# Expert weights in pages of 2 MB, each partition's 16 KB in one piece, gate and up side by side

## The chip, the cores and the metric

The kernel runs on one core of a Trainium2 chip. A core has TensorE (PE, matrix products), VectorE (DVE), ScalarE (ACT), GpSimd (POOL) and SyncE (SP, which here issues all transfers), an SBUF of 128 partitions, and 16 DMA engines that carry weights from HBM into it. The metric is the device time of one execution in microseconds (us).

## The reference

A block of attention (two kinds side by side) with a mixture of experts, and a second block of a state-space layer, a recurrent layer and two convolutional feed-forward layers; 256 tokens of 1024 features, all in fp32. The change concerns the experts of the first block:

```
N_EXPERTS = 16
EC_CAPACITY_FACTOR = 2
D_FF_EXPERT = 2 * D_MODEL

def expert_choice_ffn(h, w_router, w_gate, w_up, w_down):
    B, S, D = h.shape
    cap = EC_CAPACITY_FACTOR * S // N_EXPERTS
    aff = jax.nn.softmax((h @ w_router).astype(jnp.float32), axis=-1)
    gate, idx = lax.top_k(jnp.swapaxes(aff, 1, 2), cap)
    bidx = jnp.arange(B)[:, None, None]
    xe = h[bidx, idx]
    hid = (jax.nn.silu(jnp.einsum('becd,edf->becf', xe, w_gate))
           * jnp.einsum('becd,edf->becf', xe, w_up))
    ye = jnp.einsum('becf,efd->becd', hid, w_down) * gate[..., None].astype(h.dtype)
    return jnp.zeros_like(h).at[bidx, idx].add(ye)
```

Each of 16 experts takes 32 tokens. Its three weights, gate and up of 1024 x 2048 and down of 2048 x 1024, are 8 MB each in fp32, so the experts read 384 MB (a MB is 2^20 bytes here), each number once.

## The kernel before

The program is recorded through tile pools: a pool hands out buffers ("tiles") by tag, and a tile that takes the place of an older one makes its first writer wait until the older one's readers are done. A scheduler then orders each engine's instructions. Eight completion semaphores (DMAHW0 to DMAHW7 in the listings) are used in turn for transfers, so that a transfer waits until the eighth before it has landed.

**Pages.** Expert weights are loaded as pages of 1 MB, 8 KB for each of 128 partitions, by `load_epage` (L828 to L835). A page of gate or up is 128 rows of 2048 numbers, so that each partition gets its 8 KB as one piece. A page of down is 256 rows of 1024 numbers, two rows for each partition, two pieces of 4 KB. An expert has 24 pages: eight of gate, eight of up, eight of down.

**The ring.** The pages go into a ring of 21 places, in the order in which the room of the first block comes free: 2 in the pool `swap` (room that also holds the first half of the attention scores, `half`), 9 in `pages3`, the 5 of the pool `pages` through which the kernel loads its other weights, 4 in `pages2`, 1 in `pages4`. `pages2` to `pages4` lie where the first block kept its split weights and attention data. Page 21 goes where page 0 was, once the products with page 0 are done.

**The products of an expert** (L1065 to L1106). `xeT` holds the features of the expert's tokens along partitions. For each of the eight pages of gate, four products of 32 tokens by 512 columns go into four row groups of one accumulator, `gu0`; fp32 products run as two passes, so the profile counts eight. The same for up into `gu1`. ScalarE applies SiLU to `gu0` (L1079), VectorE multiplies by `gu1` (L1080), four transposes turn the result (`hidt`, L1083), ScalarE copies it (`hidT`, L1085), and the eight pages of down follow (`dn`, L1096). VectorE takes the result out of the accumulator with the gains (`ye`, L1099), and four products with a selection matrix add it, gated, to the tokens (`ca`, L1102). Ahead of the first expert the router picks tokens and `gather` fills `xeT` for two experts; for the other 14 it does so beside the second expert's products.

```
    ring = [(swap, "swap", 2)] * 2 + [(pages3, "page3", NP3)] * NP3 + [(pages, "page", NPAGE)] * NPAGE + \
        [(pages2, "page2", 4)] * 4 + [(pages4, "page4", 1)]
```

Of the kernel before, what the change touches and what calls it, by code (L numbers as in the profile page):

```python
# [9 lines left out]
F32 = mybir.dt.float32  # L10
# [9 lines left out]
S = 256  # L20
# [4 lines left out]
# ---------------------------------------------------------------- host layout  # L25
# [10 lines left out]
for _n, _k in COLS:  # L36
# [5 lines left out]
    # of the first block only  # L42
    ("thr", 1), ("mask0", 192), ("mask1", 192), ("invf", 1), ("sgn", 1), ("sel4", 4), ("maskp1", 128), ("maskp2", 128),
    # of all of it
# [9 lines left out]
# relative-position buckets in the order of rising key-minus-query distance, and  # L54
# the distance from which each holds
# [35 lines left out]
def column(a):  # L91
    """[..., n] vectors as columns of 128: [128, rows * n / 128]"""
    a = np.asarray(a)
    return a.reshape(-1, 128).T
# [5 lines left out]
def layout(inp):  # L100
    """the arrays of setup_inputs() as the program takes them"""
    o = {}
    cols = []
    for name, n in COLS:
        a = np.asarray(inp["b_ada" if name == "b_ada0" else name])
        if name == "b_ada0":
            # first 2048 numbers as [p, chunk, group], feature = group * 512 + chunk * 128 + p
            a = a[:, :2048].reshape(4, 4, 128).transpose(1, 0, 2)
# [42 lines left out]
    o["b_ada"] = np.asarray(inp["b_ada"]).reshape(3, 2048)  # L151
    o["a_log"] = np.asarray(inp["ssd_a_log_2"]).reshape(-1)
    skip = {"w_router", "b_ada", "w_uq", "w_ukv", "rel_bias", "positions"} | {n for n, _ in COLS}
# [7 lines left out]
def tile_model(ctx, tc, A, out):  # L161
# [28 lines left out]
    # ---------------------------------------------------------------- helpers  # L190
# [11 lines left out]
    def wpage(w, c0, n, k0=0, k=8):  # L202
        """columns c0..c0+n of rows 128*k0..128*(k0+k) of a weight"""
        return page([128, k, n], w[k0 * 128:(k0 + k) * 128, c0:c0 + n].rearrange("(k p) n -> p k n", p=128))

    def split(v, pl=None, tag="w", bufs=None, lo=None, parts=1):
        """v = hi + lo exactly, each of 12 significant bits"""
# [16 lines left out]
    def three(ps, a, b, first, last):  # L224
        """ps += a^T b for split a and b (lists over the contraction of (hi, lo) pairs)"""
# [11 lines left out]
    def inv_rms(pl, v, n, extra=None):  # L237
        """1 / sqrt(v / n + EPS) for v [128, m], the sums of n squares (m > 1: extra is None)"""
# [21 lines left out]
    def sumsq(eng, a, scratch, v):  # L260
        """v = the sums of squares over the free axis of a"""
# [7 lines left out]
    def inv_root(pl, v, n, extra=None, bias=None):  # L269
        """1 / sqrt((v + extra) / n + EPS) for v [128, 1]; bias [128, 1] takes the place of extra / n + EPS"""  # L270
# [8 lines left out]
    def root_table(pl, v):  # L279
        """the square root's table ahead of its use, from the time at which v is there"""  # L280
# [8 lines left out]
    # x1 / residual, expert inputs and rows live through several phases  # L289
    epsc = const.tile([128, 1], F32, name="epsc")  # L290
    dve.memset(epsc, EPS)
    s2c = const.tile([128, 16], F32, name="s2c")     # 1+sc2 (times gain), sh2 as columns

    # ================================================================= block 1
# [4 lines left out]
    # in the order in which their places come free  # L299
    PW = [192, 128, 128]  # L300
    # scores of the dilated heads: the first half of the heads where the first pages of the experts go
    P = [[], [], []]
    half = [swap.tile([128, 2048], F32, name="half", tag="swap", bufs=2) for _ in range(2)]
# [27 lines left out]
    W_Q0 = 704                                      # first column of the dilated heads  # L331
# [19 lines left out]
    # conditioning: one row of 6 * D numbers, four groups of columns side by side  # L351
# [4 lines left out]
    modc = act_p.tile([128, 4, 4], F32, name="modc")        # [p, chunk, group]  # L356
# [17 lines left out]
    # the rest of it, needed much later: products on the vector engine, sums over partitions at the end  # L374
# [8 lines left out]
    def mods_cols(c0, name):  # L383
        """8 * 128 of the sums as columns"""
# [6 lines left out]
    def mods_end2():  # L391
        dve.scalar_tensor_tensor(s2c[:, 0:8], mods_cols(0, "sc2"), 1.0, C("g_norm_ffn", 0, 8), ALU.add, ALU.mult)
        gt2.append(rows2.tile([128, 512], F32, name="gt2"))     # first half of the features over the second
# [11 lines left out]
    def mod_cols(j0):  # L405
        """[128, 2, 4] view of the columns of one D-vector: feature = (j - j0) * 512 + c * 128 + p"""
        return modc[:, :, j0:j0 + 2].rearrange("p c j -> p j c")
# [9 lines left out]
    # x over its norm  # L417
# [6 lines left out]
    # positions and relative-position bias, bias and band mask together  # L424
# [15 lines left out]
    def rel_bias(g, t, b):  # L440
        """bias and mask of 16 keys in each quarter of the keys of a query tile"""
# [21 lines left out]
    def tick(n=1):  # L463
        """a piece of the work that only has to be done sometime before it is needed"""
# [6 lines left out]
    # rotation angles, features along partitions (two heads of 64)  # L471
    def angles():
# [5 lines left out]
        # turns, as a multiple of 4096 and a rest  # L478
# [23 lines left out]
    def to_T(src, scol, bcol, hi, lo, pl, tpf, full=None):  # L502
        """columns of src (natural, 2 token tiles) to [features, tokens], scaled per feature, split"""
# [25 lines left out]
    # x over its norm, features along partitions  # L529
# [46 lines left out]
    # ------------------------------------------------------------ projections  # L576
    pace = [0, 1]

    def proj_T(pg, ps_of):
        """pg [128, 8, n]: for each 128 columns, [columns, tokens]"""  # L580
# [8 lines left out]
    def proj_N(pg, ps_of, tok):  # L589
        """pg [128, 8, n], or its split: [tokens, n] for the two tiles of tokens"""  # L590
# [42 lines left out]
    # gates, first half  # L633
# [18 lines left out]
    def softmax_rows(ps_view, p, den):  # L652
        """p = exp(MSC * (s - max)) for [128, 2, n] scores; den their sums"""
# [75 lines left out]
    # ------------------------------------------------------ dilated attention  # L729
# [47 lines left out]
    # weights of the three groups, in the natural order of tokens with heads along partitions  # L777
# [41 lines left out]
    # the pages of the experts, one after the other, in a ring of places  # L819
# [794 lines left out]
```

## Time and profile before

| | |
|---|---|
| median of 3 runs | 2344.3 us (2344.11 to 2346.31) |
| span of the profiled execution | 2346.6 us |
| PE busy | 2015.6 us, 86% |
| DVE, ACT, POOL busy | 937.9, 760.3, 277.5 us |
| DMA | 645.36 MB in 249,592 packets, mean 275 GB/s |
| expert pages | 3 x 128 transfers of 1024 KB, median 20 us from issue to landing |

The span runs from the first to the last instruction of one profiled execution; the page gives no other time for that execution. The experts take from about 483 us (first product) to 1408 us (last product). In the page's forms, "a<-b,c" means that an instruction writes tile a and reads b and c, and in the lists of products "x8" counts instructions that stand together. The share of the DMA is the busy time of the 16 DMA engines over the stretch; since records of neighbouring packets overlap a little, it can exceed 1. A product's busy time is partly modelled.

### The profile page before, as it was taken

What the parts mean: (1) busy time and instruction counts of PE and PEld (TensorE: products, weight loads), DVE (VectorE), ACT (ScalarE), POOL (GpSimd) and SP (SyncE); (2) the same over time, 40 slices, a digit from 0 to 9 for tenths busy, and PEclk for the clock granted to TensorE, in tenths of its full rate; (3) what the DMA queues carried; (4) which work ended last, traced back from release to release, by engine and by line L of the source; (5) the groups of instructions that cost most, each with busy time, mean ns of one, the idle gap of its engine ahead of it and who ended that gap; (6) DMA issues with size and microseconds to landing.
All of it is one profiled execution on the core that took longest, in us unless ns stands there. A gap on an engine that the chain in (4) does not pass through costs nothing. (4 is left out here: it accounts for less than half of the span.)

```text
span 2346.6 us, 32322 instructions
## 1 busy us (share of the span) xinstructions
PE 2015.6 (86%) x13779; PEld 1398.2 (60%) x13779; DVE 937.9 (40%) x1353; ACT 760.3 (32%) x1070; POOL 277.5 (12%) x209
## 2 busy tenths in 40 slices
PE   7999999998766776667676669999999999899998
PEld 5989999842111111111111119887899998799998
DVE  7866664321000000000000007665556566765565
ACT  2445453310000000000000006564555457654544
POOL 0100032000000000000000003112322222222222
PEclk9999999999676667766766779999999999999999
DMA  8358765799999999999999997333466546455652
GB/s 315 109 185 264 229 221 188 287 370 417 417 417 417 417 417 417 417 417 417 417 417 417 417 402 235 97 113 122 162 190 188 181 143 202 144 180 182 193 182 82
DMA packets 249592, 645.36 MB, mean 275 GB/s; under 512 B 10596, under 2 KB 164580, under 8 KB 213606
## 3 DMA queue, kind: packets, MB, share of 16 engines
q1 hardware_dynamic: 249448, 643.29, 73.7%
q8 instruction: 108, 1.77, 0.3%
q14 instruction: 36, 0.29, 0.0%
HBM read 641.94 MB, written 1.05 MB: 274 GB/s over the span
## 5 line engine op out<-in xcount | busy, mean ns | idle before, releaser
L219 DVE TENSOR_TENSOR wl<-page,wh 128x2048 fp32r<-128x2048 f32 (+2 forms) x191 | 431.9, 2266 | 307.6 <-ACT wh L218 307.4
L1075 PE MATMUL gu<-epage,xeT 128*32 128x512 f32 x2048 | 355.6, 785 | 149.5 <-DMA epage<-in_w_up 91.4
L218 ACT CAST wh<-page 128x2048 fp32r<-128x2048 f32 (+2 forms) x191 | 356.6, 1873 | 340.1 <-PE up L231 147.7
L1075 PEld LDWEIGHTS gu<-epage,xeT 128*32 128x32 f32 x2048 | 52.1, 121 | 429.2 <-DMA epage<-in_w_up 225.0
L230 PE MATMUL up<-hh,wh 128*128 128x256 f32 x960 | 271.7, 283 | 0.0
L232 PE MATMUL up<-hh,wl 128*128 128x256 f32 x960 | 271.7, 283 | 0.0
L231 PE MATMUL up<-hl,wh 128*128 128x256 f32 x960 | 271.7, 283 | 0.0
L1096 PE MATMUL dn<-epage,hidT 128*32 128x512 f32 x1024 | 186.3, 837 | 94.3 <-DMA epage<-in_w_down 82.7
L1080 DVE TENSOR_TENSOR hid<-hid,gu 128x512 f32<-128x512 f32 x16 | 11.0, 688 | 479.4 <-PE gu L1075 479.4
L231 PEld LDWEIGHTS up<-hl,wh 128*128 128x128 f32 x960 | 184.2, 192 | 1.0
L230 PEld LDWEIGHTS up<-hh,wh 128*128 128x128 f32 x960 | 184.2, 192 | 1.0
L232 PEld LDWEIGHTS up<-hh,wl 128*128 128x128 f32 x960 | 184.2, 192 | 0.0
L1079 ACT ACTIVATE hid<-gu 128x512 f32<-128x512 f32 x16 | 9.6, 597 | 528.4 <-PE gu L1075 528.4
L1096 PEld LDWEIGHTS dn<-epage,hidT 128*32 128x32 f32 x1024 | 27.3, 128 | 233.6 <-DMA epage<-in_w_down 201.2
L274 POOL TENSOR_SCALAR iq<-ssq 128x1 f32<-128x1 f32 x16 | 8.0, 500 | 1013.3 <-ACT x L263 975.3
L1099 DVE TENSOR_TENSOR ye<-dn,gt 128x512 f32<-128x512 f32 x16 | 11.1, 692 | 289.2 <-PE dn L1096 289.2
L1085 ACT COPY hidT<-hidt 128x512 f32<-128x512 f32 x16 | 9.4, 586 | 312.0 <-PE hidt L1083 312.0
L230 PE MATMUL qk<-hh,wh 128*128 128x256 f32 x384 | 109.9, 286 | 0.0
L231 PE MATMUL qk<-hl,wh 128*128 128x256 f32 x384 | 109.0, 284 | 0.0
L232 PE MATMUL qk<-hh,wl 128*128 128x256 f32 x384 | 108.7, 283 | 0.0
L1243 DVE SCALAR_TENSOR_TENSOR cv<-up,cols,cv 128x255 f32<-128x255 f32 x240 | 98.7, 474 | 12.5 <-ACT cv L1238 12.5
L232 PE MATMUL ca<-wh,hdl 128*128 128x512 f32 x256 | 100.1, 391 | 0.4 <-POOL hdl L219 0.4
(506 smaller groups left out, 3956.2 us busy)
## 6 DMA issues: line engine op xcount, KB each, us to landing
epage<-in_w_gate SPq DMA_DIRECT2D x128, 1024.0 KB, 20.0
epage<-in_w_up SPq DMA_DIRECT2D x128, 1024.0 KB, 19.8
epage<-in_w_down SPq DMA_DIRECT2D x128, 1024.0 KB, 19.9
page<-in_ffn_w_up SPq DMA_DIRECT2D x64, 1024.0 KB, 5.7
page<-in_w_in SPq DMA_DIRECT2D x46, 1024.0 KB, 5.4
page<-in_ffn_w_down SPq DMA_DIRECT2D x32, 1024.0 KB, 4.9
page<-in_w_ada SPq DMA_DIRECT2D x24, 1024.0 KB, 8.8
page<-in_ssd_w_in SPq DMA_DIRECT2D x20, 1024.0 KB, 5.4
```

The costliest lines, as they stand in the source:

```text
L218: act.copy(hi[p_], v[p_])
L219: (lo or dve).tensor_tensor(lw[p_], v[p_], hi[p_], ALU.subtract)
L230: pe.matmul(ps, lhsT=ah, rhs=bh, start=first and k == 0, stop=False)
L231: pe.matmul(ps, lhsT=ah, rhs=bl, start=False, stop=False)
L232: last_mm[0] = pe.matmul(ps, lhsT=al, rhs=bh, start=False, stop=last and k == n - 1)
L1075: pe.matmul(ps[32 * j:32 * j + 32, :], lhsT=xeT[:, k, 32 * e:32 * e + 32], rhs=pg[:, 0, 512 * j:512 * j + 512], start=(k == 0), stop=(k == 7))
L1079: act.activation(out=hid, in_=gu[0], func=AF.Silu)
L1080: dve.tensor_tensor(hid, hid, gu[1], ALU.mult)
L1085: act.copy(hT, pt.rearrange("p (c j s) -> p c j s", c=4, j=4))
L1096: pe.matmul(pd[32 * q:32 * q + 32, :], lhsT=hT[:, 2 * c2 + cp, j, :], rhs=pg[:, cp, 512 * n:512 * n + 512], start=(b == 0), stop=(b == 7))
L1099: dve.tensor_tensor(ye, pd, gt2, ALU.mult)
L1243: dve.scalar_tensor_tensor(y[:, c, o:], ps[:, 256 * c:256 * c + S - o], wcol(c, j), y[:, c, o:], ALU.mult, ALU.add)
```

## The change

The weights are laid out anew before the launch: `w_gu` holds, for each expert and each 128 rows, gate's 2048 and up's 2048 numbers of a row side by side, 16 KB; `w_dn` holds, for each expert and each 512 rows of down, the four rows of a partition side by side, 16 KB. A page is now 2 MB, 12 to an expert: eight of gate and up together, four of down. The ring has 10 places of 2 MB: 1 in `swap`, 4 in `pages3`, 2 that are each two of the five 1 MB tiles of the pool `pages`, 2 in `pages2`, 1 in `pages4`. A page is loaded in one transfer, but in two halves of 1 MB (8 KB of each partition) where its place is a pair of `pages` tiles, and for the last page of all. Gate's and up's products with a page follow each other, into both accumulators. `half`, the two tiles of attention scores in `swap`, become two halves of one tile. (Comments were taken out as well, which moves line numbers.)

```diff
+    gu = np.stack([np.asarray(inp[n])[0].reshape(16, 8, 128, 2048) for n in ("w_gate", "w_up")], axis=3)
+    o["w_gu"] = gu.reshape(16, 8, 128, 4096)
+    o["w_dn"] = np.asarray(inp["w_down"])[0].reshape(16, 4, 4, 128, 1024).transpose(0, 1, 3, 2, 4).reshape(16, 4, 128, 4096)
...
-    half = [swap.tile([128, 2048], F32, name="half", tag="swap", bufs=2) for _ in range(2)]
+    half = swap.tile([128, 4096], F32, name="half", tag="swap", bufs=1)
+    half = [half[:, 0:2048], half[:, 2048:4096]]
...
-    ring = [(swap, "swap", 2)] * 2
+    ring = [(swap, "swap", 1)]
     expert_pages = []
     for e in range(NE):
-        for w in (A["w_gate"], A["w_up"]):
-            expert_pages += [(w[0, e, 128 * k:128 * k + 128, :], 1) for k in range(8)]
-        expert_pages += [(A["w_down"][0, e, 256 * b:256 * b + 256, :], 2) for b in range(8)]
+        expert_pages += [A["w_gu"][e, k] for k in range(8)] + [A["w_dn"][e, b] for b in range(4)]
...
         pl, tag, nb = ring[cnt[0] % len(ring)]
-        src, a = expert_pages[cnt[0]]
+        src = expert_pages[cnt[0]]
         cnt[0] += 1
-        t = pl.tile([128, 2048], F32, name="epage", tag=tag, bufs=nb)
-        v = t.rearrange("p (a n) -> p a n", a=a)
-        last_dma[0] = sync.dma_start(out=v, in_=src.rearrange("(a p) n -> p a n", p=128))
+        if pl is pages:
+            v = [pl.tile([128, 2048], F32, name="epage", tag=tag, bufs=nb) for _ in range(2)]
+        else:
+            t = pl.tile([128, 4096], F32, name="epage", tag=tag, bufs=nb)
+            v = [t[:, :2048], t[:, 2048:]]
+        if pl is pages or cnt[0] == len(expert_pages):
+            for i in range(2):
+                last_dma[0] = sync.dma_start(out=v[i], in_=src[:, 2048 * i:2048 * i + 2048])
+        else:
+            last_dma[0] = sync.dma_start(out=t, in_=src)
         return v
...
-    pages2 = w2.enter_context(tc.tile_pool(name="pages2", bufs=4, reuse_waits="tile"))
-    pages3 = w2.enter_context(tc.tile_pool(name="pages3", bufs=NP3, reuse_waits="tile"))
+    pages2 = w2.enter_context(tc.tile_pool(name="pages2", bufs=2, reuse_waits="tile"))
+    pages3 = w2.enter_context(tc.tile_pool(name="pages3", bufs=4, reuse_waits="tile"))
     pages4 = w2.enter_context(tc.tile_pool(name="pages4", bufs=1, reuse_waits="tile"))
-    ring = [(swap, "swap", 2)] * 2 + [(pages3, "page3", NP3)] * NP3 + [(pages, "page", NPAGE)] * NPAGE + \
-        [(pages2, "page2", 4)] * 4 + [(pages4, "page4", 1)]
+    ring = [(swap, "swap", 1)] + [(pages3, "page3", 4)] * 4 + [(pages, "page", NPAGE)] * 2 + \
+        [(pages2, "page2", 2)] * 2 + [(pages4, "page4", 1)]
...
-        gu = []
-        for i, w in enumerate((A["w_gate"], A["w_up"])):
-            ps = cm(f"gu{i}")
-            for k in range(8):
-                pg = epage()
+        gu = [cm(f"gu{i}") for i in range(2)]
+        for k in range(8):
+            pg = epage()
+            for i in range(2):
                 for j in range(4):
-                    pe.matmul(ps[32 * j:32 * j + 32, :], lhsT=xeT[:, k, 32 * e:32 * e + 32],
-                              rhs=pg[:, 0, 512 * j:512 * j + 512], start=(k == 0), stop=(k == 7))
-            gu.append(ps)
+                    pe.matmul(gu[i][32 * j:32 * j + 32, :], lhsT=xeT[:, k, 32 * e:32 * e + 32],
+                              rhs=pg[i][:, 512 * j:512 * j + 512], start=(k == 0), stop=(k == 7))
...
-        for b in range(8):
+        for j in range(4):
             pg = epage()
-            j, c2 = divmod(b, 2)
-            for cp in range(2):
-                for n in range(2):
-                    q = 2 * n + cp
-                    pe.matmul(pd[32 * q:32 * q + 32, :], lhsT=hT[:, 2 * c2 + cp, j, :],
-                              rhs=pg[:, cp, 512 * n:512 * n + 512], start=(b == 0), stop=(b == 7))
+            for c2 in range(2):
+                for cp in range(2):
+                    for n in range(2):
+                        q = 2 * n + cp
+                        o = 1024 * cp + 512 * n
+                        pe.matmul(pd[32 * q:32 * q + 32, :], lhsT=hT[:, 2 * c2 + cp, j, :], rhs=pg[c2][:, o:o + 512],
+                                  start=(j == 0 and c2 == 0), stop=(j == 3 and c2 == 1))
```

SyncE's list where the ring fills for the first time, before: the last places of `page3` and `pages`, then the five of `pages2` and `pages4`, then the first page that waits for products of an expert.

```order
L834 DMA epage<-in_w_up 128x2048 [waits DMAHW0_49]
L834 DMA epage<-in_w_up 128x2048 [waits DMAHW1_49,DVE_49]
L834 DMA epage<-in_w_up 128x2048 [waits DMAHW2_49,DVE_49]
L834 DMA epage<-in_w_down 128x2x1024 [waits DMAHW3_49,PE_49]
L834 DMA epage<-in_w_down 128x2x1024 [waits DMAHW4_49]
L834 DMA epage<-in_w_down 128x2x1024 [waits DMAHW5_49]
L834 DMA epage<-in_w_down 128x2x1024 [waits DMAHW6_49]
L834 DMA epage<-in_w_down 128x2x1024 [waits DMAHW7_49,DVE_49]
L834 DMA epage<-in_w_down 128x2x1024 [waits DMAHW0_49,PE_49]
```

The same place of SyncE's list after the change, where `in_w_gu` is gate and up and `in_w_dn` is down:

```order
L845 DMA epage<-in_w_gu 128x4096 [waits DMAHW2_49]
L843 DMA epage<-in_w_gu 128x2048 [waits DVE_49]
L845 DMA epage<-in_w_gu 128x4096 [waits DMAHW4_49,DVE_49,PE_49]
L845 DMA epage<-in_w_dn 128x4096 [waits DMAHW5_49]
L845 DMA epage<-in_w_dn 128x4096 [waits DMAHW6_49,DVE_49]
L845 DMA epage<-in_w_dn 128x4096 [waits DMAHW7_49,PE_49]
```

Three transfers of 2 MB instead of five of 1 MB fill `pages2` and `pages4`, and one tile of `pages` is filled ahead of them where two were; the next row waits for the products with page 0 in both.

TensorE's list around the end of an expert's gate and up, before: the last two pages of up (one accumulator, `gu_6110`), the transposes, the first page of down.

```order
L1075 MATMUL gu_6110<-epage,xeT 32x512 [waits DMAHW1_49]
L1075 MATMUL gu_6110<-epage,xeT 32x512 x3
L1075 MATMUL gu_6110<-epage,xeT 32x512 [waits DMAHW2_49]
L1075 MATMUL gu_6110<-epage,xeT 32x512 x3
L1083 MATMUL hidt<-kc,hid 128x128 [waits DVE_49]
L1083 MATMUL hidt<-kc,hid 128x128 x3
L1096 MATMUL dn<-epage,hidT 32x512 [waits DMAHW3_49,Activation_49]
L1096 MATMUL dn<-epage,hidT 32x512 x3
```

The same place after the change, with gate's accumulator `gu_5854` and up's `gu_5855`:

```order
L1084 MATMUL gu_5854<-epage,xeT 32x512 [waits DMAHW7_49]
L1084 MATMUL gu_5854<-epage,xeT 32x512 x3
L1084 MATMUL gu_5855<-epage,xeT 32x512 x4
L1084 MATMUL gu_5854<-epage,xeT 32x512 [waits DMAHW0_49]
L1084 MATMUL gu_5854<-epage,xeT 32x512 x3
L1084 MATMUL gu_5855<-epage,xeT 32x512 x4
L1091 MATMUL hidt<-kc,hid 128x128 [waits DVE_49]
L1091 MATMUL hidt<-kc,hid 128x128 x3
L1105 MATMUL dn<-epage,hidT 32x512 [waits DMAHW1_49,Activation_49]
L1105 MATMUL dn<-epage,hidT 32x512 x7
```

One wait for a landed page now stands ahead of eight products instead of four, and gate's sum is complete only with the last page, four products ahead of up's.

SyncE's list at the end of the experts, before: the last pages, three small loads, and the first weights of the second block.

```order
L834 DMA epage<-in_w_down 128x2x1024 [waits DMAHW1_49,PE_49]
L834 DMA epage<-in_w_down 128x2x1024 [waits DMAHW2_49,PE_49]
L1124 DMA cols_8231<-in_cols 128x766 [waits DMAHW3_49,PE_49]
L1114 DMA row<-in_g_final 128x1024 [waits DMAHW4_49]
L1114 DMA rowa<-in_norm_mix_pre 128x1024 [waits DMAHW5_49]
L199 DMA page<-in_ssd_w_dt 128x8x128 [waits DMAHW6_49,PE_49]
L199 DMA page<-in_ssd_w_in 128x8x256 [waits DMAHW7_49,PE_49]
```

The same place after the change:

```order
L845 DMA epage<-in_w_dn 128x4096 [waits DMAHW7_49,PE_49]
L843 DMA epage<-in_w_dn 128x2048 [waits DMAHW0_49,PE_49]
L843 DMA epage<-in_w_dn 128x2048 [waits DMAHW1_49]
L1133 DMA cols_7923<-in_cols 128x766 [waits DMAHW2_49,PE_49]
L1123 DMA row<-in_g_final 128x1024 [waits DMAHW3_49]
L1123 DMA rowa<-in_norm_mix_pre 128x1024 [waits DMAHW4_49]
L203 DMA page<-in_ssd_w_dt 128x8x128 [waits DMAHW5_49]
L203 DMA page<-in_ssd_w_in 128x8x256 [waits DMAHW6_49,PE_49]
```

The order is the same; the last page is in two transfers, and the first weights of the second block no longer wait for TensorE.

## Rows read from the trace of the kernel before

**Rows 1.** The page: GB/s moved by DMA in 40 slices of 58.7 us

```profile
GB/s 315 109 185 264 229 221 188 287 370 417 417 417 417 417 417 417 417 417 417 417 417 417 417 402 235 97 113 122 162 190 188 181 143 202 144 180 182 193 182 82
```

**Rows 2.** The DMA queue's own waits: total us, times, longest us

```profile
SPq L834 <- DMA epage<-in_w_gate: 255.3, 121, 3.4
SPq L834 <- DMA epage<-in_w_down: 135.5, 80, 3.4
SPq L834 <- DMA epage<-in_w_up: 133.6, 75, 2.5
SPq L834 <- PE gu L1075: 79.4, 66, 16.7
```

**Rows 3.** Groups of instructions, 547 to 1404 us: busy us, mean ns, idle before

```profile
L1075 PE MATMUL gu<-epage,xeT 128*32 128x512 f32 x1824 | 323.4, 808 | 149.5 <-DMA epage<-in_w_up 91.4 <-DMA epage<-in_w_gate 57.8
L1096 PE MATMUL dn<-epage,hidT 128*32 128x512 f32 x956 | 178.2, 853 | 93.7 <-DMA epage<-in_w_down 82.7 <-ACT hidT L1085 11.0
L1102 PE MATMUL ca<-ye,sel 128*128 128x512 f32 x112 | 75.3, 833 | 11.4 <-DVE ye L1099 11.4
```

**Rows 4.** Timeline within one expert: start us, us, instruction, idle before and releaser

```profile
820.43 0.60 ACT L1079 ACTIVATE hid<-gu 128x512 f32<-128x512 f32 x1 [37.72 <-PE gu L1075]
...
823.40 1.94 PE L1075 MATMUL gu<-epage,xeT 128*32 128x512 f32 x8 [0.46 <-DMA epage<-in_w_up]
...
838.31 1.93 PE L1075 MATMUL gu<-epage,xeT 128*32 128x512 f32 x8 [0.55 <-DMA epage<-in_w_up]
...
840.38 0.69 DVE L1080 TENSOR_TENSOR hid<-hid,gu 128x512 f32<-128x512 f32 x1 [32.88 <-PE gu L1075]
...
842.98 4.13 PE L1096 MATMUL dn<-epage,hidT 128*32 128x512 f32 x24 [0.73 <-ACT hidT L1085]
...
848.54 1.07 PE L1096 MATMUL dn<-epage,hidT 128*32 128x512 f32 x8 [1.44 <-DMA epage<-in_w_down]
...
858.76 1.94 PE L1096 MATMUL dn<-epage,hidT 128*32 128x512 f32 x8 [0.62 <-DMA epage<-in_w_down]
```

**Rows 5.** Windows: us, engines' busy us, TensorE's clock, DMA share, GB/s

```profile
846.00:856.20 10.20, 5.18 (x36) 0.71 (x32) 0.00 (x0) 0.00 (x0) 0.00 (x0) 0.82 1.03 410
864.00:878.60 14.60, 10.93 (x62) 2.60 (x60) 0.74 (x2) 0.00 (x0) 0.00 (x0) 0.85 1.01 422
1430.00:1438.00 8.00, 8.00 (x69) 8.00 (x68) 5.51 (x11) 6.33 (x7) 5.22 (x11) 1.00 1.09 354
```

**Rows 6.** DMA: a queue's packets, MB, share; issues with median us to landing

```profile
q8 instruction: 108, 1.77, 0.3%
...
page<-in_ffn_w_up SPq DMA_DIRECT2D x64, 1024.0 KB, 5.7
...
page<-in_ssd_w_in SPq DMA_DIRECT2D x20, 1024.0 KB, 5.4
```

**Rows 7.** The line that issues expert pages, L834

```profile
DMA to landing us min/median/max: 4.8/19.9/21.6
```

**Rows 8.** Timeline at the first expert, of SyncE's queue and of TensorE

```profile
464.58 21.65 SPq L834 DMA_DIRECT2D epage<-in_w_down  x8
...
483.01 13.94 PE L1075 MATMUL gu<-epage,xeT 128*32 128x512 f32 x128
```

**Rows 9.** Windows ahead of the first expert

```profile
457.00:464.00 7.00, 6.93 (x58) 6.55 (x57) 1.45 (x3) 1.50 (x5) 0.00 (x0) 1.00 0.75 311
...
480.00:487.00 7.00, 7.00 (x68) 4.21 (x71) 2.54 (x9) 2.90 (x5) 0.00 (x0) 1.00 0.25 68
```

**Rows 10.** Timeline at the end of the experts

```profile
1393.70 0.66 SPq L199 DMA_DIRECT2D page<-in_ssd_w_dt  x1
...
1403.89 1.86 PE L1096 MATMUL dn<-epage,hidT 128*32 128x512 f32 x8 [0.59 <-DMA epage<-in_w_down]
...
1414.82 7.70 PE L1140 MATMUL lead<-hf,page 128*128 128x128 f32 x48
```

More of the change, by code (lines that the diff above doesn't have):

```diff
@@ L151, in layout @@
     o["b_ada"] = np.asarray(inp["b_ada"]).reshape(3, 2048)
+    gu = np.stack([np.asarray(inp[n])[0].reshape(16, 8, 128, 2048) for n in ("w_gate", "w_up")], axis=3)
+    o["w_gu"] = gu.reshape(16, 8, 128, 4096)
+    o["w_dn"] = np.asarray(inp["w_down"])[0].reshape(16, 4, 4, 128, 1024).transpose(0, 1, 3, 2, 4).reshape(16, 4, 128, 4096)
     o["a_log"] = np.asarray(inp["ssd_a_log_2"]).reshape(-1)
-    skip = {"w_router", "b_ada", "w_uq", "w_ukv", "rel_bias", "positions"} | {n for n, _ in COLS}
+    skip = {"w_gate", "w_up", "w_down", "w_router", "b_ada", "w_uq", "w_ukv", "rel_bias", "positions"} | {n for n, _ in COLS}
     for n, a in inp.items():
@@ L842, in tile_model @@
             with tc.issue_after(last_dma[0].ins):
-                ahead += [load_epage() for _ in range(2)]
+                ahead.append(load_epage())
             behind = last_dma[0]
@@ L956, in tile_model @@
     sp_.close()
-    NP3 = 9
     w2 = ctx.enter_context(ExitStack())
-    pages2 = w2.enter_context(tc.tile_pool(name="pages2", bufs=4, reuse_waits="tile"))
-    pages3 = w2.enter_context(tc.tile_pool(name="pages3", bufs=NP3, reuse_waits="tile"))
+    pages2 = w2.enter_context(tc.tile_pool(name="pages2", bufs=2, reuse_waits="tile"))
+    pages3 = w2.enter_context(tc.tile_pool(name="pages3", bufs=4, reuse_waits="tile"))
     pages4 = w2.enter_context(tc.tile_pool(name="pages4", bufs=1, reuse_waits="tile"))
-    ring = [(swap, "swap", 2)] * 2 + [(pages3, "page3", NP3)] * NP3 + [(pages, "page", NPAGE)] * NPAGE + \
-        [(pages2, "page2", 4)] * 4 + [(pages4, "page4", 1)]
+    ring = [(swap, "swap", 1)] + [(pages3, "page3", 4)] * 4 + [(pages, "page", NPAGE)] * 2 + \
+        [(pages2, "page2", 2)] * 2 + [(pages4, "page4", 1)]
     xps_ = ctx.enter_context(ExitStack())
```

## The prediction

> **What bounds the kernel now.** The row of moved bytes by slice of the page comes first [rows 1]: from about 490 us to 1400 us of the 2346.6 us the 16 DMA engines move 417 GB/s, slice after slice. That is the expert stretch. The page's chain of work says little about it, since it breaks off where the work waits for DMA, so I went on with the queue's own waits [rows 2]: SyncE, which issues the pages, waits mostly until an earlier page has landed (255.3 + 135.5 + 133.6 us), far less for TensorE to free a place (79.4 us). TensorE's products in the stretch take 323.4 + 178.2 + 75.3 = 577 us of 857 us [rows 3]. So the stretch ends when the last byte has landed, and TensorE, VectorE and ScalarE have room.
>
> How fast pages land is read from TensorE's starts, since it waits for each page [rows 4]. Gate and up: six pages from 823.40 to 838.31, 2.485 us for 1 MB. Down: four pages from 848.54 to 858.76, 2.555 us. The same megabyte takes 0.070 us longer when a partition's 8 KB come as two pieces of 4 KB. The windows say the same: 422 GB/s while gate and up arrive, 410 GB/s with down, the engines' share above 1.0 in both [rows 5].
>
> **What a piece costs.** Each engine carries 64 KB of a page: eight pieces of 8 KB at 2.485/8 = 310.6 ns, or sixteen of 4 KB at 2.555/16 = 159.7 ns. A straight line through the two: 37.7 ns per KB and 8.8 ns for the piece itself. It can be tested on a third size: where the second block loads weight rows of 1 KB with the engines full, the line gives 46.5 ns a piece, 16 x 1024 B / 46.5 ns = 352 GB/s, and the window shows 354 [rows 5]. So I let the line hold to 16 KB: 612.4 ns a piece, eight of them per engine in 2 MB, 4.899 us a page, 2.450 us per MB.
>
> The trace has no weight piece of 16 KB. From below, the line without its 8.8 ns gives 4.83 us a page. From above stand two rows: 8 KB pieces, as before, give 4.970 us, and the only 16 KB packets in the trace, 108 packets of 1.77 MB of instructions, used 0.3% of 16 engines' 2346.6 us, some 1.04 us each [rows 6]. Those do not go where weights go, and the three sizes on the line do, so I take the line. The Trainium skill (HBM Reference, Specifications) gives a core that streams alone about 425 GB/s; the trace is already at 422 with 8 KB pieces. By the page 1 MB would never take under 2.467 us, an estimate by which the changed kernel would stand near 2333 us.
>
> **The change part by part.**
>
> *The steady stretch.* Two of each ten ring places are pairs of 1 MB tiles, loaded as two transfers whose pieces are still 8 KB, and so is the very last page; these cost 2 x 2.485 = 4.970 us. At the restart of the stream (below) 21 pages of 1 MB are in place before, ten of 2 MB after. Before: 363 to come, 123 of down and 240 of gate and up, 123 x 2.555 + 240 x 2.485 = 910.7 us. After: 182 to come, 37 in halves and 145 whole, 37 x 4.970 + 145 x 4.899 = 894.3 us. Saved: 16.4 us, the megabyte that the shorter ring holds less already counted. (The rows show some 917 us from 487 to 1403.89 [rows 9, 10]; the 6 us beyond my 910.7 I leave in both.)
>
> *The start.* All places fill before TensorE uses a page. The last five places come free at 464.58 [rows 8], when the first block's last products are done; at 2.5 us a page they are full by about 480, and the DMA runs at 68 GB/s from 480 to 487 [rows 9], until TensorE frees the first place. It starts on the experts at 483.01 and does 128 products in 13.94 us [rows 8], so the first place is free after eight products, 0.87 us. Afterwards the first place is 2 MB and wants sixteen, so the stream comes back 0.87 us later. An earlier pause grows: 14 MB of places are to be had ahead of 464.58 instead of 16, so the DMA, dry near the end of 457 to 464 now (311 GB/s [rows 9]), runs dry 5 us sooner; but 6 MB instead of 5 follow, in by about 482, still before the first place is free. That pause thus costs nothing beyond the megabyte counted. Net so far 16.4 - 0.9 = 15.5 us.
>
> *Gate and up side by side.* Before, SiLU of gate (0.60 us) ran while up was landing [rows 4]; now it follows the last page, ahead of the product with up, the transposes and down. That is about 0.7 us more of pause on TensorE per expert, 11 us over sixteen if nothing hid it. It is hidden: TensorE has 280 us to spare in the stretch, and DMA goes on through the pause, because about 20 us of transfers are in the queue (median to landing 19.9 us [rows 7]). At the last expert too: after up come the down pages, four of 4.9 us.
>
> *The ring.* Eight transfers are in flight at a time: each issue waits for the eighth before it, which gives 8 x 2.5 = 20 us. Before, 21 places less 8 in flight let TensorE lag 13 pages, 32 us. After, in the mean 1.2 transfers per page, so eight are 6.7 pages of ten, and a lag of 3.3 pages, 16 us, is free; more only thins the queue of about 32 us. TensorE's longest pauses, the gated products at an expert's end (75.3 us over 14 experts, 5.4 us each [rows 3]) and the 3.3 us from the last up product to down (2.6 us from 840.38 to 842.97 [rows 4] and the 0.7 us), stay under that even when they add. I cost it at nothing; if the cover were gone, it is the fourth case below.
>
> *The end.* The last page is loaded in halves, so the last eight products wait for 1 MB, as now (1.86 us at 1403.89 [rows 10]). The loads of the second block are issued as before behind the last pages (SyncE at 1393.70), and its first products start at 1414.82, 11 us after the last page [rows 10]; nothing is added there. What follows is the same list of work, with a few neighbours in another order: 2 us either way.
>
> *Sum.* The profiled span of 2346.6 us falls to 2331.1 us. That execution lies 2.3 us above the median of the runs, 2344.3 us, so the median should be 2328.8 us, 0.66% less. Runs of this kernel lie within 2.2 us of one another, so 0.2% (4.7 us) is about what can be told from no change.
>
> **Rivals.**
>
> *Pieces of 16 KB go at the rate of 8 KB pieces* (the piece is cut in two, or something else than the piece caps the stream). For it: nothing above 422 GB/s is seen. Against it: three sizes on one line. All 182 pages cost 4.970 us, 904.5 us; saved 910.7 - 904.5 - 0.9 = 5.3 us: 2339.0 us. The Trainium skill (DMA: Bandwidth & Descriptors, Rules for kernel authors) asks for at least 1 MiB per DMA for full bandwidth, which the kernel before already has; by that rule larger transfers bring nothing, which is this case.
>
> *Slower: 16 KB pieces are dearer than the line.* Neighbouring rows lie 16 KB apart in memory, where they lay 8 or 4 KB apart. For it: the 1.04 us of the instruction packets [rows 6], and rows 32 KB apart (the up projection of the feed-forward) take 5.7 us to land where rows 20 KB apart (the second block's first projection) take 5.4 [rows 6], 5.6% more. Against it: 4 and 8 KB fit one line although their distances differ. It decides when the 145 whole pages lose 15.5 us, 0.107 us each: a piece of 626 ns instead of 612, 2.2% more. At 5.6% more they lose 39.8 us: 2369 us. (With 1.04 us a piece it would be near 2820 us, which I do not believe.) The Trainium skill (DMA: Bandwidth & Descriptors, Latency and other measured facts) has copies slow down at row pitches of large powers of two, from 512 KiB on, and would lay tiles out contiguously; no run here shows a pitch of that size.
>
> *The coarse ring starves the queue.* Places come free in steps of 2 MB, ten of them. For it: SyncE already waits 66 times for gate and up products [rows 2]. Against it: the 20 us in flight. If it cost 1 us per expert, all would be lost: 2344 us.
>
> **How the numbers follow.** The line: 0.62, 2319 to 2335 us (on one side a piece without its 8.8 ns, 145 x 0.07 = 10 us; on the other a start 4 us dearer than worked out and 2 us from the second block's order). Rate of 8 KB: 0.18. Starved queue: 0.11. Dearer pieces: 0.09. Predicted is the line's 2329 us. The range 2320 to 2342 us reaches to the second case and leaves out the dearer pieces and most of the starved queue. Faster by over 0.2% (under 2339.6 us): the line and somewhat over half of the second case, 0.74. Same: the rest of it and most of the third, 0.15. Slower: 0.11.
>
> **What would show it.** Right: whole pages land 4.90 us apart; about 427 GB/s through the stretch (24 MB in 9.6 x 4.899 + 2.4 x 4.970 = 58.96 us an expert, before 60.20); weight packets fall from 65,536 (one per piece) to 29,568; the DMA idles from about 458 to 467 and 482 to 487. The second case shows 4.97 us and 422 GB/s. Dearer pieces show over 5.0 us with the DMA share at 1. A starved queue shows a share under 1 in mid-stretch and SyncE waiting for TensorE. I am wrong outright if the stretch shortens as said and the second block grows by as much.

## The result, and the profile after

The changed kernel takes 2324.7 us (median of 4 runs, 2323.6 to 2326.5) beside 2344.2 us for the kernel before, measured along with it: 0.9919 of it, 95% interval 0.9905 to 0.9932; the medians lie 19.5 us apart. Two further measurements, below, give 0.9917 and 0.9933 (17.6 and 15.0 us less by the medians). Forecast were 15.5 us less, 2329 us, with a range from 2320 to 2342 us.

The page of the changed kernel answers to [rows 1]: GB/s moved by DMA in 40 slices (58.1 us each now), and the packets.

```profile
GB/s 318 110 184 262 228 222 197 241 383 427 427 426 426 425 427 427 427 426 426 427 426 427 427 402 214 94 143 91 182 187 191 184 132 199 145 183 189 191 181 82
DMA packets 211173, 645.32 MB, mean 278 GB/s; under 512 B 8148, under 2 KB 162132, under 8 KB 178390
```

The level stretch stands at 425 to 427 GB/s where it stood at 417, and it is still level: the kernel is bound by the same stream. The pitch at which pages land is seen in the timeline of TensorE in the changed kernel (start us, us, instruction, idle before and its releaser), as in [rows 4]; the first three rows are halves of pages that come in two transfers, the others whole pages.

```profile
810.32 1.06 PE L1084 MATMUL gu<-epage,xeT 128*32 128x512 f32 x8 [0.66 <-DMA epage<-in_w_gu]
812.81 1.07 PE L1084 MATMUL gu<-epage,xeT 128*32 128x512 f32 x8 [1.43 <-DMA epage<-in_w_gu]
815.29 1.07 PE L1084 MATMUL gu<-epage,xeT 128*32 128x512 f32 x8 [1.42 <-DMA epage<-in_w_gu]
...
871.88 3.37 PE L1084 MATMUL gu<-epage,xeT 128*32 128x512 f32 x16 [3.34 <-DMA epage<-in_w_gu]
876.77 1.92 PE L1084 MATMUL gu<-epage,xeT 128*32 128x512 f32 x16 [1.52 <-DMA epage<-in_w_gu]
881.67 3.59 PE L1084 MATMUL gu<-epage,xeT 128*32 128x512 f32 x16 [2.98 <-DMA epage<-in_w_gu]
886.57 1.92 PE L1084 MATMUL gu<-epage,xeT 128*32 128x512 f32 x16 [1.31 <-DMA epage<-in_w_gu]
891.47 3.26 PE L1084 MATMUL gu<-epage,xeT 128*32 128x512 f32 x16 [2.98 <-DMA epage<-in_w_gu]
```

Four whole pages take 891.47 - 871.88 = 19.59 us, 4.90 us each; a half takes (815.29 - 810.32)/2 = 2.485 us, as a page of gate did before. Every page shown is waited for, whether its 16 products took 1.92 us or 3.59 us.

The windows of the changed kernel (us, busy us of the engines, TensorE's clock, DMA share, GB/s) show the start, which answers to [rows 9], and the stretch:

```profile
457.00:464.00 7.00, 5.82 (x49) 5.42 (x47) 1.00 (x2) 1.16 (x5) 0.00 (x0) 1.00 0.11 21
...
467.00:480.00 13.00, 10.23 (x39) 6.06 (x38) 9.03 (x39) 4.09 (x9) 0.00 (x0) 0.67 0.95 407
480.00:487.00 7.00, 7.00 (x69) 3.02 (x72) 1.71 (x7) 2.09 (x3) 0.00 (x0) 1.00 0.40 116
548.00:1383.00 835.00, 508.92 (x2904) 112.40 (x2908) 29.70 (x57) 18.43 (x30) 0.00 (x0) 0.81 1.01 426
```

The stretch of the kernel before, for comparison:

```profile
548.00:1403.00 855.00, 587.79 (x2940) 108.13 (x2932) 30.31 (x57) 18.43 (x30) 0.00 (x0) 0.71 1.02 417
```

The earlier pause is there (21 GB/s from 457 to 464), and the last pages loaded ahead still land before TensorE begins on the experts. The queue's own waits, in answer to [rows 2], with the row of the kernel before (L834) that [rows 2] does not show, and the timeline at both ends of the stretch, in answer to [rows 8, 10]:

```profile
SPq L845 <- DMA epage<-in_w_gu: 306.1, 91, 4.8
...
SPq L845 <- PE gu L1084: 35.2, 10, 19.1
```

```profile
SPq L834 <- PE dn L1096: 61.5, 33, 4.1
```

```profile
481.31 10.94 PE L1084 MATMUL gu<-epage,xeT 128*32 128x512 f32 x100
...
1385.47 1.06 PE L1105 MATMUL dn<-epage,hidT 128*32 128x512 f32 x8 [0.78 <-DMA epage<-in_w_dn]
...
1395.61 0.80 PE L1149 MATMUL lead<-hf,page 128*128 128x128 f32 x2
```

SyncE waits for the expert products less than before, not more: 35.2 us for those of gate and up where it was 79.4, and 0.5 us for those of down where it was 61.5. From the first expert product to the end of the last one the stretch took 1403.89 + 1.86 - 483.01 = 922.7 us before [rows 8, 10] and 1385.47 + 1.06 - 481.31 = 905.2 us now: 17.5 us. That is the measure that I use below, since it leaves out what varies ahead of it and behind it.

### The profile page after: what moved, and what is told of

It is laid out like the page before. It is cut to its first block, busy times and chain, and to the rows that moved or that the text cites. A ratio compares the mean times of both kernels' runs of the same rounds, so it can differ in the third digit from the quotient of the medians.

```text
span 2324.5 us, 31982 instructions
## 1 busy us (share of the span) xinstructions
PE 1935.0 (83%) x13779; PEld 1398.8 (60%) x13779; DVE 937.7 (40%) x1353; ACT 760.1 (33%) x1070; POOL 277.6 (12%) x209
## 2 busy tenths in 40 slices
DMA packets 211173, 645.32 MB, mean 278 GB/s; under 512 B 8148, under 2 KB 162132, under 8 KB 178390
## 5 line engine op out<-in xcount | busy, mean ns | idle before, releaser
L1084 PE MATMUL gu<-epage,xeT 128*32 128x512 f32 x2048 | 318.0, 739 | 193.3 <-DMA epage<-in_w_gu 193.2
L1084 PEld LDWEIGHTS gu<-epage,xeT 128*32 128x32 f32 x2048 | 60.8, 122 | 430.3 <-DMA epage<-in_w_gu 322.9
L1105 PE MATMUL dn<-epage,hidT 128*32 128x512 f32 x1024 | 164.5, 772 | 110.4 <-DMA epage<-in_w_dn 101.6
L1252 DVE SCALAR_TENSOR_TENSOR cv<-up,cols,cv 128x255 f32<-128x255 f32 x240 | 98.7, 474 | 11.6 <-ACT cv L1247 11.6
L235 PE MATMUL ca<-wl,hdh 128*128 128x512 f32 x256 | 100.2, 391 | 0.0
## 6 DMA issues: line engine op xcount, KB each, us to landing
epage<-in_w_gu SPq DMA_DIRECT2D x102, 2048.0 KB, 29.6
```

The source lines that it names most:

```text
L235: pe.matmul(ps, lhsT=ah, rhs=bl, start=False, stop=False)
L1084: pe.matmul(gu[i][32 * j:32 * j + 32, :], lhsT=xeT[:, k, 32 * e:32 * e + 32], rhs=pg[i][:, 512 * j:512 * j + 512], start=(k == 0), stop=(k ...
L1105: pe.matmul(pd[32 * q:32 * q + 32, :], lhsT=hT[:, 2 * c2 + cp, j, :], rhs=pg[c2][:, o:o + 512], start=(j == 0 and c2 == 0), stop=(j == 3 a ...
L1252: dve.scalar_tensor_tensor(y[:, c, o:], ps[:, 256 * c:256 * c + S - o], wcol(c, j), y[:, c, o:], ALU.mult, ALU.add)
```

## The experiments

The theory: time goes by the pieces, 8.8 ns for each and 37.7 ns per KB, and nothing else in the change counts. The rivals: the size of a transfer, the order of the products, or the ring gave the gain.

**Every page in two transfers.** The changed kernel, with 1 MB a transfer and 8 KB a piece:

```diff
-        if pl is pages or cnt[0] == len(expert_pages):
+        if True:
             for i in range(2):
                 last_dma[0] = sync.dma_start(out=v[i], in_=src[:, 2048 * i:2048 * i + 2048])
```

> The changed kernel with every page in two transfers of 1 MB (pieces of 8 KB), the layout, the side-by-side order and the ring as they are. If time goes by the number of pieces (8.8 ns a piece and 37.7 ns a KB), 145 whole pages go from 4.899 to 4.970 us: +10.3 us, some 2335 us, pages 4.97 us apart at 422 GB/s. If the gain came from the layout, the order of the products or the ring, nothing changes: 2323 to 2327 us.

2338.8 us beside 2344.6 before: 0.9976 (0.9963 to 0.9988), 5.7 us less by the medians where the forecast's 15.5 and this 10.3 leave 5.2. In a window and two neighbouring halves of pages in its timeline:

```profile
548.00:1395.00 847.00, 574.72 (x2916) 101.89 (x2916) 30.29 (x57) 18.42 (x30) 0.00 (x0) 0.74 1.01 421
```

```profile
878.45 1.07 PE L1084 MATMUL gu<-epage,xeT 128*32 128x512 f32 x8 [0.97 <-DMA epage<-in_w_gu]
880.94 1.06 PE L1084 MATMUL gu<-epage,xeT 128*32 128x512 f32 x8 [1.42 <-DMA epage<-in_w_gu]
```

421 GB/s and 2.49 us for half a page: layout, order and ring are those of the change, and two thirds of the gain are gone. This run changes transfers and pieces together, so the next keeps the transfers.

**Transfers of 2 MB in pieces of 4 KB.** The changed kernel with another layout in memory, so that a page is 4 x 128 pieces:

```diff
-    o["w_gu"] = gu.reshape(16, 8, 128, 4096)
+    o["w_gu"] = gu.reshape(16, 8, 128, 4, 1024).transpose(0, 1, 3, 2, 4)
...
-            last_dma[0] = sync.dma_start(out=t, in_=src)
+            last_dma[0] = sync.dma_start(out=t.rearrange("p (a n) -> p a n", a=4), in_=src.rearrange("a p n -> p a n"))
```

> The changed kernel with its transfers and pages of 2 MB as they are, but the weights laid out so that a page is 512 pieces of 4 KB. By the line of piece sizes a page takes 32 x 159.6 ns = 5.11 us: 182 pages, +36 to +38 us, some 2361 us, slower than the kernel before, whose pieces are two thirds 8 KB. If the size of a transfer were what counts, nothing changes: 2323 to 2327 us.

2361.8 us, 1.0068 of before (1.0049 to 1.0087): slower than the kernel before by 17 us by the medians, as large as its transfers are. Timeline and window:

```profile
890.87 3.23 PE L1084 MATMUL gu<-epage,xeT 128*32 128x512 f32 x16 [4.05 <-DMA epage<-in_w_gu]
895.98 1.92 PE L1084 MATMUL gu<-epage,xeT 128*32 128x512 f32 x16 [1.88 <-DMA epage<-in_w_gu]
```

```profile
548.00:1425.00 877.00, 518.53 (x2936) 111.93 (x2928) 30.27 (x57) 19.02 (x31) 0.00 (x0) 0.80 1.02 409
```

A page takes 895.98 - 890.87 = 5.11 us, the line's number, and twice the 2.555 us that 1 MB took before in the same pieces of 4 KB: a transfer of twice the size changed nothing. The size of the transfer is out as a cause.

**Down alone in pieces of 8 KB.** The kernel before with one array laid out anew:

```diff
+    o["w_dn"] = np.asarray(inp["w_down"])[0].reshape(16, 8, 2, 128, 1024).transpose(0, 1, 3, 2, 4).reshape(16, 8, 128, 2048)
...
-        last_dma[0] = sync.dma_start(out=v, in_=src.rearrange("(a p) n -> p a n", p=128))
+        last_dma[0] = sync.dma_start(out=t, in_=src)
```

> The kernel before with one thing changed: the down weights lie so that a 1 MB page gives each partition one piece of 8 KB in place of two of 4 KB. By the line 123 pages gain 0.070 us each: -8.6 us, some 2335.6 us, and the pages of down as far apart as those of gate and up (2.485 us). If 4 KB pieces had cost nothing, 2344 us.

2336.2 us beside 2344.6: 0.9964 (0.9949 to 0.9980), 8.4 us less, 8.6 forecast. Its down pages in the timeline, where [rows 4] had 2.555 us:

```profile
903.95 1.07 PE L1097 MATMUL dn<-epage,hidT 128*32 128x512 f32 x8 [1.42 <-DMA epage<-in_w_dn]
906.43 1.06 PE L1097 MATMUL dn<-epage,hidT 128*32 128x512 f32 x8 [1.42 <-DMA epage<-in_w_dn]
908.92 1.07 PE L1097 MATMUL dn<-epage,hidT 128*32 128x512 f32 x8 [1.43 <-DMA epage<-in_w_dn]
```

**Side by side alone.** The kernel before, its gate and up pages alternating:

```diff
-        for w in (A["w_gate"], A["w_up"]):
-            expert_pages += [(w[0, e, 128 * k:128 * k + 128, :], 1) for k in range(8)]
+        expert_pages += [(w[0, e, 128 * k:128 * k + 128, :], 1) for k in range(8) for w in (A["w_gate"], A["w_up"])]
...
+        for k in range(8):
+            for i in range(2):
                 pg = epage()
```

> The kernel before with one thing changed: pages of gate and up alternate and are multiplied side by side. If the products are hidden under the stream: no change, 2343 to 2346 us. If the pause after the last product of gate and up had been covered by the products of up before, and is not now: +11 us, some 2355 us. TensorE's granted clock in the stretch of the experts stays at 0.71 if the clock goes by how the pages come, and rises towards 0.81 if it goes by the order of the products.

2344.2 beside 2344.6 us, 0.9998 (0.9987 to 1.0009): nothing. The stretch is the same 417 GB/s at the same granted clock of 0.71:

```profile
548.00:1403.00 855.00, 590.20 (x2932) 107.19 (x2924) 30.29 (x57) 19.02 (x31) 0.00 (x0) 0.71 1.02 417
```

**Smaller rings.** The changed kernel with nine places and with six in place of ten; the edit of the second:

```diff
-    ring = [(swap, "swap", 1)] + [(pages3, "page3", 4)] * 4 + [(pages, "page", NPAGE)] * 2 + \
-        [(pages2, "page2", 2)] * 2 + [(pages4, "page4", 1)]
+    ring = [(swap, "swap", 1)] + [(pages3, "page3", 2)] * 2 + [(pages, "page", NPAGE)] * 2 + \
+        [(pages2, "page2", 1)] * 1 + [(pages4, "page4", 1)] * 0
```

> The changed kernel with one place of 2 MB less in the ring (nine). If the ring counts only in that it is loaded ahead before the experts start: the 2 MB loaded ahead less come at 426 GB/s within the stretch, +4.9 us, some 2330 us, the stream at 426 GB/s. If the coarse ring is near to starving the queue: more than +8 us, and SyncE's waits on TensorE grow well beyond the 35 us that they have.

> The changed kernel with a ring of six places, 12 MB. If the ring counts only by what is loaded ahead: four pages of 4.9 us more within the stretch, +19.6 us, some 2344 us, the stream still at 426 GB/s with a DMA share of 1.0. If fewer places starve the queue: more than +25 us, a share of DMA below 1.0 and SyncE's waits on TensorE by the hundred us.

Nine places: 2333.2 us, beside 2326.9 for the changed kernel on the same chip, 6.4 us more. Six: 2349.7, 22.9 us more. Most of both is what is no longer loaded ahead, 4.9 and 19.6 us; the smaller rings also give the halves a larger share (two of six places instead of two of ten, some 62 of 186 pages, which adds 25 x 0.07 = 1.8 us). Some 1.5 us of each are not accounted for. The six places in a window and in the queue's waits:

```profile
548.00:1407.00 859.00, 544.38 (x3040) 122.02 (x3039) 31.66 (x61) 20.63 (x35) 0.00 (x0) 0.77 1.01 424
```

```profile
SPq L845 <- PE gu L1084: 311.3, 92, 19.2
SPq L845 <- PE dn L1105: 112.8, 30, 12.2
```

SyncE now waits more than 400 us for TensorE, and yet the DMA share is 1.01 and the stream has 424 GB/s. My expectation took such waits for a sign of starvation, and there it was wrong: a wait of the issuing engine says only which of two limits came last; whether the queue ran dry is read from the DMA share. Even 12 MB of places keep the stream fed, so ten did all the more.

**Pieces of 32 KB.** The changed kernel, with 108 pages in pairs: two pages interleaved in memory, one transfer of 4 MB each, in a place that comes free after the second page:

```diff
+    for n in range(191):
+        if n % 10 in (1, 3, 7):
+            wx[n:n + 2] = wx[n:n + 2].transpose(1, 0, 2).reshape(2, 128, 4096)
...
+            t = pl.tile([128, 8192], F32, name="epage", tag=tag, bufs=nb)
...
+            last_dma[0] = sync.dma_start(out=t, in_=two)
```

> The changed kernel with 108 of the pages loaded in pairs, one transfer of 4 MB with a piece of 32 KB for each partition. By the line a piece takes 1215 ns and a pair 9.72 us in place of 9.80: 54 pairs, -4 us, some 2320 us. If the cost of a piece no longer counts above 16 KB: 2325 us. If a pair's place, which comes free only after its second page, starves the queue: above 2330 us.

2326.3 beside 2326.9 us for the changed kernel: no gain in time. Yet the timeline has the pairs as the line has them, 9.72 us from the second of these rows to the third (9.78 from the first), and the stretch took 901.3 us, 4 less. The 4 us went behind the experts, where 12.3 us pass from the end of the last expert product to the second block's first product, beside 9.1 us in the changed kernel's trace:

```profile
876.31 6.82 PE L1101 MATMUL gu<-epage,xeT 128*32 128x512 f32 x48 [5.34 <-DMA epage<-in_w_x]
886.09 3.53 PE L1101 MATMUL gu<-epage,xeT 128*32 128x512 f32 x16 [2.96 <-DMA epage<-in_w_x]
895.81 3.64 PE L1101 MATMUL gu<-epage,xeT 128*32 128x512 f32 x16 [6.19 <-DMA epage<-in_w_x]
...
1383.90 0.33 SPq L1150 DMA_DIRECT2D cols<-in_cols  x1
...
1389.98 1.29 DVE L1187 TENSOR_TENSOR xg<-ca,row 128x512 f32<-128x512 f32 x2 [5.38 <-DMA rowa<-in_norm_mix_pre]
```

The second block's first rows wait for the place of 4 MB that the last expert page had. They are issued at 1383.90, after the last expert product, and VectorE waits 5.38 us for one of them. In the changed kernel the same load was issued behind the last page, 27 us ahead of the last eight expert products, as its timeline of SyncE's queue shows:

```profile
1358.41 0.33 SPq L1133 DMA_DIRECT2D cols<-in_cols  x1
```

**Pairs, with the last page elsewhere.** The same kernel, its last page in the places of the halves:

```diff
-        if len(ring) > 1 and pl is pages3 and cnt[0] == len(expert_pages):
-            t = pl.tile([128, 8192], F32, name="epage", tag=tag, bufs=nb)
-            v = [t[:, :2048], t[:, 2048:4096]]
-        elif pl is pages:
+        if cnt[0] == len(expert_pages):
+            pl, tag, nb = pages, "page", NPAGE
+        if pl is pages:
```

> The kernel with pairs of pages, with the last page in two of the 1 MB places and not in a place of 4 MB. In the kernel with pairs the stretch of the experts was 4 us shorter, as the line has it, but the first rows of the second block shared the last page's place, were issued at 1383.90, after the last product of the experts, and VectorE waited 5.38 us for one of them. If that is where the 4 us went, they are issued about 20 us earlier here, the wait is gone, and the time is some 3 us below that of the changed kernel (2322 to 2324 us beside 2326). If the pair's places cost the time elsewhere, no change against the pairs: as the changed kernel within 1 us.

2320.0 us (2318.9 to 2320.7) beside 2326.8 us (2325.7 to 2327.3) for the changed kernel on the same chip and 2341.8 for the kernel before: 0.9903 of before (0.9888 to 0.9918). It beats both. In its trace the loads stand early and the wait is gone:

```profile
1352.43 0.42 SPq L1149 DMA_DIRECT2D cols<-in_cols  x1
...
1384.53 0.69 DVE L1186 TENSOR_TENSOR xg<-ca,row 128x512 f32<-128x512 f32 x1 [1.94 <-ACT x L272]
```

The medians differ by 6.8 us, where 3 were expected; between the two profiled executions it is 2323.6 - 2318.5 = 5.1 us of span, 3.8 of them in the stretch (905.3 and 901.5 us). The rest of the 6.8 us is not accounted for.

**The changed kernel again**, twice, for the size of the difference, beside the two kernels with pairs:

> The changed kernel once more, for the size of the difference: -15.5 us as forecast, or -19 us as first measured. If the 1.2 us of the first block and the 3 us at the start of the second block, which no step of the forecast had, are scatter of one execution, this profile shows them otherwise; if they go with the change, they are there again.

> The changed kernel a third time, beside the one above on the same chip: 2324 to 2327 us. If the start of the experts (481.3 and 483.8 in two executions of this kernel) and the clock after them are scatter, they take other values again.

2326.9 us, 0.9917 of before (0.9903 to 0.9930), and 2326.8 us, 0.9933 (0.9920 to 0.9947). The profile of the first of them, at both ends of the stretch, then that of the second:

```profile
483.79 2.78 PE L1084 MATMUL gu<-epage,xeT 128*32 128x512 f32 x24
...
1387.89 1.94 PE L1105 MATMUL dn<-epage,hidT 128*32 128x512 f32 x8 [1.44 <-DMA epage<-in_w_dn]
...
1400.23 1.05 PE L1149 MATMUL lead<-hf,page 128*128 128x128 f32 x7
```

```profile
480.47 5.79 PE L1084 MATMUL gu<-epage,xeT 128*32 128x512 f32 x52
...
1384.71 1.06 PE L1105 MATMUL dn<-epage,hidT 128*32 128x512 f32 x8 [0.76 <-DMA epage<-in_w_dn]
...
1394.84 1.44 PE L1149 MATMUL lead<-hf,page 128*128 128x128 f32 x5
```

The experts start at 481.3, 483.8 and 480.5 us in three executions of one kernel, and at 483.0 before: that was scatter. The stretch repeats: 905.2, 906.0 and 905.3 us. From the second block's first product to the end it is 928.9, 928.1 and 928.8 us, beside 931.8 before; what that is worth is told under the size, below.

## Why the prediction was right, step by step

*The line* held at the size that it was made for, and at two others. Whole pages: 4.90 us where 4.899 was worked out; pieces of 4 KB in 2 MB transfers: 5.11 for 5.107; of 32 KB: 9.72 to 9.78 us for 9.722. In all profiled executions, from the first expert product to the end of the last one, and from the second block's first product to the end of the span:

| kernel | stretch of the experts, us | second block, us |
|---|---|---|
| before | 922.7 | 931.8 |
| side by side alone | 922.7 | 931.7 |
| down alone in 8 KB | 913.9 | 925.1 |
| changed, three executions | 905.2, 906.0, 905.3 | 928.9, 928.1, 928.8 |
| every page in halves | 917.1 | 928.3 |
| 2 MB in pieces of 4 KB | 944.0 | 928.3 |
| nine places | 912.7 | 928.5 |
| six places | 926.4 | 925.1 |
| pairs in pieces of 32 KB | 901.3 | 928.9 |
| pairs, last page elsewhere | 901.5 | 928.1 |

The stretch moved by -17.2 us for the change (mean of three), -8.9 for down alone, and against the changed kernel +11.6 with 8 KB, +38.5 with 4 KB and -4.2 with 32 KB, where the line has -15.5 with the later restart, -8.6, +10.3, +35.2 (182 x 5.107 less 894.3) and -4.1. With 8 and 4 KB it came out 12% and 9% above the line; 0.6 us of each are the last eight products, which took 1.93 us there and 1.06 us in two of three executions of the changed kernel. The remainder is not accounted for.

*The first rival*, 16 KB at the rate of 8 KB, is out by the 4.90 us. The window has 426 GB/s over the stretch, 427 and 428 with the pairs, and 1 MB takes 2.45 us. The Trainium skill (HBM Reference, Specifications) has about 425 GB/s for a lone core, by which 1 MB would take no less than an estimated 2.467 us: the measurement is a little faster, and it decides. The Trainium skill's rule of at least 1 MiB per DMA (DMA: Bandwidth & Descriptors, Rules for kernel authors) is kept by all these kernels and does not tell them apart: with all transfers at 1 or 2 MB the stream had 409, 421 or 426 GB/s, by the piece.

*Dearer pieces*, the rival on the other side, is out by the same rows: contiguous rows of 16 KB bear no penalty, and of 32 KB neither. *The coarse ring* is out by the share of 1.01, with six places too.

*Side by side* cost nothing, alone or in the change; the 20 us in the queue cover the longer pause (some 30 us after the change, where a whole page lands 29.6 us after its issue in the median). *The start* came as said but for a few us of shift: SyncE's first issue into a freed place stood at 484.14 before, 1.13 us after the first product, and at 483.30 now, 1.99 us after it, 0.86 us more where 0.87 was forecast. *Weight packets* were to fall by 35,968. All packets fell by 249,592 - 211,173 = 38,419; of the other 2,451, 2,448 are small ones (below).

*The waits.* The prediction's reading of [rows 2] put the waits for TensorE at 79.4 us. That left out the 61.5 us for products of down; with them it is 140.9 us beside some 524 us for landed pages. The bound was read rightly even so, as the DMA share of 1.02 in the stretch before shows.

*The size.* The sum gave 15.5 us; three measurements have 19.5, 17.6 and 15.0 us by the medians, 17.4 in the mean. One term was a little too small: the stretch gave 17.2 us. Of the 1.7 us over the forecast, 0.5 are the last eight products, which ran at the full clock in two of three executions (1.06 us, before 1.86), and that was luck; up to the start of those eight the stretch shortened by 16.7 us (16.6 to 16.8 in the three). The remaining 1.2 us are not accounted for.

"Nothing is added" at the end, with 2 us either way for the second block, is not contradicted. The profiled execution before took 931.8 us there, some 3 us more than the changed kernel, but the table's last column does not follow the change: 931.7 with side by side alone, 925.1 with down alone and with six places. The profiled execution before was also a long one. In each run with both numbers the time is 1.7 to 2.3 us above the span, so its span of 2346.6 us stands for some 2349 us (an estimate), about 4.5 us above the median; the prediction compared the span itself with the median and took 2.3 us, which does not alter the forecast difference. And the scatter of the kernel before is larger than the 2.2 us that the prediction took from three runs: 24 later runs on one chip lie between 2338.7 and 2349.1 us.

TensorE's clock has a part in the second block's length. Rows of its first 8 us, before, after the change (first execution), after the change (second), and with down alone:

```profile
1414.82:1422.82 8.00, 8.00 (x54) 8.00 (x54) 7.07 (x8) 3.76 (x7) 2.96 (x2) 0.73 0.11 34
```

```profile
1395.61:1403.61 8.00, 7.76 (x62) 7.53 (x62) 7.34 (x9) 4.94 (x10) 2.95 (x2) 0.91 0.22 66
```

```profile
1400.23:1408.23 8.00, 7.76 (x65) 7.35 (x66) 7.69 (x9) 5.41 (x10) 3.30 (x3) 1.00 0.04 11
```

```profile
1404.07:1412.07 8.00, 7.76 (x65) 7.36 (x66) 7.70 (x9) 5.40 (x10) 3.31 (x3) 1.00 0.04 10
```

TensorE comes to these products out of a stretch in which it was busy 60 to 70% of the time and went back and forth between 1.2 and 2.4 GHz; at which of the two it arrives differs between executions of one kernel (0.91 and 1.00). Between the first two rows that makes some 1.4 us (the first 48 `lead` products took 7.70 us [rows 10] and 6.32 us); it is not what makes 3 us. The last two rows both have 1.00, and their second blocks took 928.1 and 925.1 us. They part for good only some 600 us later, where the granted clock is 0.86 in the one and 0.93 in the other:

```profile
2010.23:2060.23 50.00, 41.09 (x226) 35.99 (x227) 31.30 (x30) 25.71 (x40) 12.30 (x11) 0.86 0.33 106
```

```profile
2014.07:2064.07 50.00, 41.04 (x253) 36.42 (x254) 32.81 (x31) 26.65 (x42) 12.61 (x11) 0.93 0.37 115
```

Why the clock differs there, and whether the change has any share in it, no run shows.

## What to carry to other kernels

Where a profile shows a level stretch with the DMA share at 1, as here, ask whether the bound is the engines' time for pieces: take the durations of two piece sizes from the trace, draw the line, and try it on a third size before a layout is changed; a larger transfer alone moved nothing here. Laying one array out anew (down, half of the gain in a few lines) can be tried ahead of the rest. When a buffer is made coarser, look at what is loaded into its memory next: the pairs won 4 us in the stream and lost them to a row that waited for the last page's place. And do not read a few microseconds of a later stage from one profiled execution: compare several kernels that leave that stage alone.

## What the runs showed of the hardware

A transfer brings small packets of its own. The changed kernel issues its expert pages in 231 transfers instead of 384, and the page's count of packets under 512 B falls from 10,596 to 8,148: 2,448, which is 153 x 16, as many for each transfer as there are DMA engines. With every page in halves it is 10,596 again:

```profile
DMA packets 233206, 645.34 MB, mean 276 GB/s; under 512 B 10596, under 2 KB 164580, under 8 KB 180838
```

TensorE's granted clock in the stretch differs for the same products: 0.71 before and side by side and 0.74 with halves, where 8 products mostly follow one another; 0.81 in the changed kernel and 0.80 with 4 KB pieces, where it is mostly 16; 0.78 with the pairs, where it is up to 48. The order of the products does not set it, as side by side alone shows; what does was not tried. The groups of the changed kernel show it in the mean time of one product, beside 808, 853 and 833 ns in [rows 3]. Over all the products of the experts TensorE is busy for 551.8 us where it was 624.6, some 73 us less, in a stretch that does not wait for it.

```profile
L1084 PE MATMUL gu<-epage,xeT 128*32 128x512 f32 x1796 | 283.7, 759 | 193.3 <-DMA epage<-in_w_gu 193.2
L1105 PE MATMUL dn<-epage,hidT 128*32 128x512 f32 x940 | 154.9, 787 | 109.0 <-DMA epage<-in_w_dn 100.8 <-ACT hidT L1093 8.0
L1111 PE MATMUL ca<-ye,sel 128*128 128x512 f32 x112 | 61.9, 703 | 11.4 <-DVE ye L1108 11.4
```
